# A two-layer decoder trunk on one core: norm rows asked for elsewhere, indices behind the first product, the first expert pair by halves

## The chip, the cores and the metric

The kernel runs on one core of one Trainium2 chip. A core has TensorE (PE: matrix products, with PEld for its weight loads), VectorE (DVE), ScalarE (ACT), GpSimd (POOL), the queue of SyncE (SP), and 16 DMA engines that move data between HBM and the on-chip memory. The metric is the device time of one execution in microseconds, the median of the runs.

## The reference

The reference is a decoder trunk of two layers for 256 tokens of 1024 features. Each layer mixes tokens (a gated linear recurrence in the first layer, stick-breaking attention in the second, both beside a softmax attention to 256 memory tokens), projects, adds and normalizes, and then applies a mixture of experts, adds and normalizes. Cut to the part that the change touches:

```python
mixed = jnp.concatenate([seq_out, mem_out], axis=-1)
x = post_norm(x, mixed @ w_o[layer], ln_mix_g[layer], ln_mix_b[layer])     # LN(alpha*x + out) * g + b
probs_g = softmax(xf @ w_group + b_group); p_top, g_idx = top_k(probs_g, 1)      # one of 4 groups
w_top, e_local = top_k(softmax(logits of that group), 2)                       # two of its 4 experts
h = silu(einsum('td,edf->tef', xf, w_gate)) * einsum('td,edf->tef', xf, w_up)   # 256 inner features
y = einsum('tef,efd->td', h * gates[:, :, None], w_down)                       # 16 experts
x = post_norm(x, y, ln_ffn_g[layer], ln_ffn_b[layer])
```

## The kernel before

The program is one unrolled stream of instructions per engine. A planner (the Tile scheduler) orders the instructions of each engine by program order and a simulated time; inside `tc.manual_schedule`, and for instructions given to `pin`, the written order stands. Tiles with one tag share a buffer, and a new tile waits for the readers of the old one.

**Weights.** All weights lie in one array of chunks of 1 MB. `Stream` (L54) sends them in order on SP's queue into free buffers: nine of a ring, and others that stages open for a time with `stream.open(names, end)`, for chunks below `end`. A chunk waits for the chunk that was sent three before it to land (DEPTH, L29, L96) and for its buffer. An expert pair has six chunks: four of gate and up weights (two halves of the 1024 features for each of two experts), two of down weights. The second layer's experts are the last 48 chunks; its last one is the last transfer of weights of the program.

**Routing, in `mixer_end`** (L937). TensorE finishes the output projection; VectorE adds the residual in four pieces (`add`, L399), two per tile of 128 tokens; `turn_in` (L561) transposes the sum four blocks at a time into PSUM, ScalarE copies them to `sT` (L567), and `logits` (L569) multiplies by the router's weights, while the norm's variance goes from VectorE (L409 or L423) to GpSimd, which raises it to the power -0.5 (L410, L424), and back to VectorE (L413, L427). `rank` and `pick` (L576, L593) on VectorE choose the experts, `count` (L600) on TensorE numbers the slots, `place` and `slots` (L607, L617) on VectorE build one-hot blocks `P0` (pair 0) and `P1` (all pairs). `z` (L960) writes the normalized rows to HBM. `gather_first` (L635) makes pair 0's transposed rows with products with `P0`, one call per tile of tokens. In the second layer the order of these on VectorE, TensorE and ScalarE is written by hand from L1016 to L1059.

**After it** (L1066 to L1081), `indices` (L653) multiplies all one-hot blocks by the token numbers (16 products of one column), VectorE makes integers of them, and GpSimd fetches pair 1 and 2 by indirect DMA. `first_rows` (L647) applies the norm's gain and bias to pair 0's eight blocks, four on ScalarE (L629) and four on VectorE (L627). `rows` (L376) brings the norm's two rows of 1024 into one partition of the tile `gb`, by ScalarE's queue, and GpSimd broadcasts each to 128 partitions (L384); with `by_transfer` one DMA of 1 MB repeats them instead (L380). `affine` (L432) multiplies and adds with them on VectorE.

**Experts, in `Moe.run`** (L803). Eight pairs of experts, 64 slots each. For each pair `gu` makes gate and up (512 columns, 256 of each, in one PSUM bank), 8 blocks of features by two experts; a product of 32-bit numbers runs as two instructions. ScalarE takes silu of the gate (L873), VectorE multiplies by up and by the slot's gate value (L875) to `h`; TensorE transposes `h` (L899), ScalarE copies it (L900), and the down products (L913) make two halves of 512 outputs. Pair 0 already takes ScalarE's and VectorE's work on `h` in two halves of 128 features. `turn` (L764) gets the gate values of a pair; `transpose_rows` (L782) turns the next pair's fetched rows. Pairs 5 to 7 are combined by products (L828), the others by way of HBM. All PE instructions of this part are pinned. `beyond` (L486) is for more than 64 tokens at an expert; every engine loads a number for it (L488), SP too.

The tile `gb` (tag "gb") is first the gate of the recurrence, then the norm rows, and in the second layer the value tile `vB` (read last by `so`, L1566). Slots "x0" and "x1" hold the layer's transposed input until the last projection has read it, and weights afterwards.

## Time and profile before

| | us |
|---|---|
| median of 3 runs | 525.6 (524.14 to 529.12) |
| the profiled execution, its own time | 526.96 |
| span of that execution, first to last instruction | 525.3 |
| TensorE busy | 491.1 |
| VectorE busy | 300.2 |
| ScalarE busy | 229.6 |
| GpSimd busy | 62.9 |
| data moved by DMA | 161.61 MB, 308 GB/s on the mean |

The profile lists each instruction with its start, counted from the first instruction, and its duration; an engine's idle time before an instruction stands in brackets with what ended it. The duration of a product contains its latency, so products in a row overlap and a row of several (x16) covers less than the sum. "issue" says that the engine waited for nothing that the profile shows. Issues of DMA stand on the queue of the engine that makes them (SPq, ACTq, POOLq), and their duration there is that of the issue, not of the transfer. The granted clock is a share of 2.4 GHz.

### The profile page before, as it was taken

How to read it: one execution, taken by the hardware profiler on the slowest of the kernel's cores; microseconds unless marked ns; L12 is line 12 of the kernel's file. 1: busy time of each engine (PE TensorE's matmuls, PEld its weight loads, DVE VectorE, ACT ScalarE, POOL GpSimd, SP SyncE). 2: the span in 40 equal slices, each digit the busy share in tenths (PEclk: the TensorE clock that was granted, in tenths of full speed). 3: DMA queues.
4: the chain of work that ended last, by engine and by line, in shares of the span. 5: the costliest groups of instructions: out<-in, count | busy, mean ns of one | idle time of the engine just before them, and what ended most of it. 6: DMA issues, size and time to landing. Idle time of an engine off the chain costs nothing. (4 is left out here: it accounts for less than half of the span.)

```text
span 525.3 us, 9096 instructions
## 1 busy us (share of the span) xinstructions
PE 491.1 (93%) x3534; PEld 326.7 (62%) x3534; DVE 300.2 (57%) x682; ACT 229.6 (44%) x471; POOL 62.9 (12%) x78
## 2 busy tenths in 40 slices
PE   4999999999999999999797999998998899999992
PEld 4998898788996333333236889877687333333431
DVE  4668876867758622233338698677445842233547
ACT  4845446684445222333017566668423232222322
POOL 1100000002132111112011500000010121111201
PEclk9999999999999999999898999999998999999997
DMA  8999834447888999999999763242999799999922
GB/s 270 407 404 404 345 103 160 161 156 326 299 332 321 384 403 384 394 385 407 409 379 395 271 252 143 100 160 99 381 365 364 288 382 419 414 422 409 412 119 81
DMA packets 28439, 161.61 MB, mean 308 GB/s; under 512 B 5239, under 2 KB 5623, under 8 KB 11363
## 3 DMA queue, kind: packets, MB, share of 16 engines
q1 hardware_dynamic: 20736, 140.76, 68.3%
q0 software_dynamic: 4752, 10.94, 5.4%
q10 hardware_dynamic: 2902, 9.26, 4.8%
q8 instruction: 30, 0.49, 0.4%
q14 instruction: 19, 0.16, 0.1%
HBM read 158.92 MB, written 13.64 MB: 329 GB/s over the span
## 5 line engine op out<-in xcount | busy, mean ns | idle before, releaser
L820 PE MATMUL gu<-w,ex 128*64 128x512 f32 x256 | 62.9, 609 | 3.4 <-DMA w<-in_w_all_dram 2.3
L820 PE MATMUL gu<-w,xg 128*64 128x512 f32 x256 | 60.8, 601 | 0.1
L913 PE MATMUL po<-w,hT 128*64 128x512 f32 (+1 forms) x272 | 58.4, 570 | 0.1
L913 PEld LDWEIGHTS po<-w,hT 128*64 128x64 f32 x272 | 18.8, 136 | 34.0 <-issue 27.3
L820 PEld LDWEIGHTS gu<-w,ex 128*64 128x64 f32 x256 | 17.2, 137 | 34.8 <-issue 26.1
L820 PEld LDWEIGHTS gu<-w,xg 128*64 128x64 f32 x256 | 16.4, 136 | 26.5 <-issue 24.6
L920 DVE COPY hr<-po 128x512 f32<-128x512 f32 x10 | 6.9, 692 | 43.1 <-PE po L913 43.0
L629 ACT ACTIVATE xg<-xgp,lnT 128x128 f32<-128x128 f32 x32 | 13.5, 457 | 25.6 <-PE xgp L791 22.4
L918 DVE TENSOR_TENSOR hl<-po,hl 128x512 fp32r<-128x512 f32 (+1 forms) x14 | 8.5, 615 | 26.5 <-ACT hl L917 25.5
L627 DVE TENSOR_SCALAR xg<-xgp,lnT 128x128 f32<-128x128 f32 x32 | 12.4, 408 | 19.0 <-ACT xg L629 15.7
L629 ACT ACTIVATE ex<-xgp,lnT 128x128 f32<-128x128 f32 x32 | 14.3, 458 | 19.3 <-PE xgp L791 19.0
L627 DVE TENSOR_SCALAR ex<-xgp,lnT 128x128 f32<-128x128 f32 x32 | 13.1, 410 | 15.1 <-ACT ex L629 13.9
L900 ACT ACTIVATE hT<-ht 128x256 f32<-128x256 f32 (+1 forms) x18 | 6.5, 360 | 34.4 <-PE ht L899 34.3
L873 ACT ACTIVATE h<-gu 128x256 f32<-128x256 f32 (+1 forms) x18 | 6.3, 360 | 34.3 <-PE gu L820 34.3
L234 DVE TENSOR_TENSOR wo<-w,wo 128x512 fp32r<-128x512 f32 x20 | 13.7, 727 | 10.8 <-ACT wo L226 10.8
L760 POOL DMA_INDIRECT hd<-hr,own x10 | 10.1, 1014 | 81.2 <-DVE gsl L780 76.3
L673 POOL DMA_INDIRECT zg<-zd,idx x14 | 14.6, 1041 | 43.2 <-PE xgp L791 25.1
L791 PEld LDWEIGHTS xgp<-cst,zg 128*128 128x128 f32 x112 | 12.0, 141 | 11.4 <-PE gu L820 7.3
L1291 POOL TENSOR_TENSOR rms<-rms,neghalf 128x2 f32<-128x2 f32 x6 | 4.1, 699 | 111.6 <-ACT sq L1287 99.4
L384 POOL PARTITION_BROADCAST gbm<-gbm x4 | 5.3, 1398 | 94.2 <-DMA gbm<-in_ln_dram 85.5
L226 ACT ACTIVATE wo<-w 128x512 fp32r<-128x512 f32 x20 | 11.5, 628 | 9.8 <-PE wo L472 8.2
L917 ACT ACTIVATE hl<-po 128x512 fp32r<-128x512 f32 (+1 forms) x14 | 7.5, 537 | 18.4 <-PE po L913 18.4
(462 smaller groups left out, 1357.7 us busy)
## 6 DMA issues: line engine op xcount, KB each, us to landing
w<-in_w_all_dram SPq DMA_DIRECT2D x131, 1024.0 KB
hd<-in_w_all_dram ACTq DMA_DIRECT2D x2, 2560.0 KB
w<-in_w_all_dram SPq DMA_DIRECT2D x6, 256.0 KB
x_tok<-in_x_tok_dram ACTq DMA_DIRECT2D x1, 1024.0 KB
zd<-z ACTq DMA_DIRECT2D x2, 512.0 KB
gbo<-in_ln_dram ACTq DMA_DIRECT2D x1, 1024.0 KB
out_dram<-z SPq DMA_DIRECT2D x4, 256.0 KB
w<-in_w_all_dram SPq DMA_DIRECT2D x1, 512.0 KB
```

The costliest lines, as they stand in the source:

```text
L226: self.last_hi = nc.scalar.activation(p[:, 0, s], src[:, s], AF.Copy, scale=1.0 if scale is None else scale).ins
L234: nc.vector.tensor_sub(p[:, 1, s], src[:, s], p[:, 0, s])
L627: ins = nc.vector.tensor_scalar(xg[:, kk], ps, g, b, op0=ALU.mult, op1=ALU.add)
L629: nc.scalar.activation(xg[:, kk], ps, AF.Identity, scale=g, bias=b)
L673: nc.gpsimd.indirect_dma_start(out=self.zg[:, p % 2], out_offset=None, in_=self.zd, in_offset=bass.IndirectOffsetOnAxis(ap=self.idx[:, p:p ...
L760: pin(nc.gpsimd.indirect_dma_start(out=self.hd, out_offset=bass.IndirectOffsetOnAxis(ap=self.own[:, p:p + 1], axis=0), in_=src, in_offset= ...
L791: pin(nc.tensor.transpose(ps[:, k], self.zg[:, p % 2, (4 * hk + k) * P:(4 * hk + k + 1) * P], ident))
L820: pin(nc.tensor.matmul(gus[p][c * 64:(c + 1) * 64], xgs[p][:, kk, c * CAP:(c + 1) * CAP], ws[p][2 * kh + c][0][:, k * 512:(k + 1) * 512], ...
L913: pin(nc.tensor.matmul(po[c * 64:(c + 1) * 64], hT[:, f, c * 64:(c + 1) * 64], ws[p][4 + c][0][:, f * D + s.start:f * D + s.stop], start=( ...
L917: self.hl_last = nc.scalar.activation(hl[:, 0, s], po, AF.Copy).ins
L918: pin(nc.vector.tensor_sub(hl[:, 1, s], po, hl[:, 0, s]))
L920: nc.vector.tensor_copy(hr[:, p % 2, s], po)
```

## The change

The diff has these parts.

- `rows` can fill a tile that is handed to it. The first layer's norm rows (of the mixer's norm) are asked for ahead of the load of `x_tok`; the second layer's by the repeating transfer, into slot "x1", behind the value projection and ahead of the output projection. `mixer_end` takes them as an argument, and no longer asks for them behind `first_rows`.
- In the second layer, "x1" is no longer opened for weights ahead of the output projection; "gb" is opened when the heads are done, and "x1" when `affine` has read it.
- `turn_in` copies the last of its four groups (second tile, second half) in two copies of two blocks.
- `first_rows` gives all eight blocks to ScalarE.
- `indices` is called behind the first block of pair 0's gate and up products, and its products are pinned.
- Pair 0's gate and up columns are read in the order gate, up, gate, up of 128 each (by the access pattern of the weights); the last four blocks of features are done first for the first 256 columns, then for the second 256.
- Pair 0's down products: both output halves with the first 128 inner features right behind the first half of `h`, with the second 128 behind the second half.

```diff
--- before.py
+++ after.py
@@ -373,9 +373,9 @@
     def tok_tile(which, name):
         return keep.tile([P, NT, D], F32, tag=which, name=name)
 
-    def rows(which, name, by_transfer=False):
-
-        gb = tok_tile("gb", f"gb{name}")
+    def rows(which, name, by_transfer=False, gb=None):
+
+        gb = tok_tile("gb", f"gb{name}") if gb is None else gb
         if by_transfer:
             nc.scalar.dma_start(gb, ln_d[0, 2 * which:2 * which + 2].partition_broadcast(P))
             return gb
@@ -562,9 +562,12 @@
 
             ps = bank(f"zt{self.l}", tag="y", shape=(P, 4, P))
             sT = self.sT[t, hk] = self.tmp.tile([P, 4, P], F32, tag="sT", name=f"sT{self.l}{t}", bufs=2)
+
+            n = 2 if t == hk == 1 else 4
             for k in range(4):
                 nc.tensor.transpose(ps[:, k], s[:, t, (4 * hk + k) * P:(4 * hk + k + 1) * P], ident)
-            nc.scalar.activation(sT, ps, AF.Copy)
+                if k % n == n - 1:
+                    nc.scalar.activation(sT[:, k + 1 - n:k + 1], ps[:, k + 1 - n:k + 1], AF.Copy)
 
         def logits(self, t, hk):
             if hk == 0:
@@ -647,7 +650,7 @@
         def first_rows(self):
             xg = self.work.tile([P, NK, P], F32, tag="xg", name=f"xg{self.l}")
             for k in range(NK):
-                self.features(xg, self.first[k // 4][:, k % 4], k, k // 4)
+                self.features(xg, self.first[k // 4][:, k % 4], k, 0)
             return xg
 
         def indices(self):
@@ -658,8 +661,8 @@
             ps = bank(f"idx{l}", tag="m", shape=(P, 8))
             for p in range(8):
                 for t in range(NT):
-                    nc.tensor.matmul(ps[:, p:p + 1], self.P1f[:, t, p * P:(p + 1) * P], tokb[:, t:t + 1], start=(t == 0),
-                                     stop=(t == 1))
+                    pin(nc.tensor.matmul(ps[:, p:p + 1], self.P1f[:, t, p * P:(p + 1) * P], tokb[:, t:t + 1],
+                                         start=(t == 0), stop=(t == 1)))
 
 
             pin(nc.vector.tensor_scalar(self.idx[:, 0:3], ps[:, 0:3], float(T), T - 1.0, op0=ALU.add, op1=ALU.min))
@@ -809,7 +812,7 @@
 
             quarters = [slice(0, 512), slice(512, 768), slice(768, D)]
 
-            def gu(p, ks):
+            def gu(p, ks, part=slice(0, 512)):
 
                 if p not in ws:
                     ws[p] = [stream.get() for _ in range(6)]
@@ -817,10 +820,13 @@
                 for kk in ks:
                     kh, k = kk // 4, kk % 4
                     for c in range(2):
-                        pin(nc.tensor.matmul(gus[p][c * 64:(c + 1) * 64], xgs[p][:, kk, c * CAP:(c + 1) * CAP],
-                                            ws[p][2 * kh + c][0][:, k * 512:(k + 1) * 512], start=(kk == 0),
-                                            stop=(kk == NK - 1)))
-                    if k == 3:
+                        w = ws[p][2 * kh + c][0][:, k * 512:(k + 1) * 512]
+                        if p == 0:
+                            w = w.rearrange("p (g h n) -> p h g n", g=2, h=2)
+                            w = w if part.stop - part.start == 512 else w[:, part.start // 256]
+                        pin(nc.tensor.matmul(gus[p][c * 64:(c + 1) * 64, part], xgs[p][:, kk, c * CAP:(c + 1) * CAP],
+                                            w, start=(kk == 0), stop=(kk == NK - 1), skip_group_check=(p == 0)))
+                    if k == 3 and part.stop == 512:
                         stream.done(ws[p][2 * kh][1], ws[p][2 * kh + 1][1])
 
             def combine(p, t, s):
@@ -835,10 +841,13 @@
 
             for p in range(8):
                 if p == 0:
-                    gu(0, range(4))
+                    gu(0, range(1))
+                    self.indices()
+                    gu(0, range(1, 4))
                     self.gates()
                     self.turn(0)
-                    gu(0, range(4, 8))
+                    for j in range(2):
+                        gu(0, range(4, 8), slice(256 * j, 256 * j + 256))
                     self.ex = slots.tile([P, 2, D], F32, tag="ex", name=f"ex{l}")
                 else:
 
@@ -869,11 +878,14 @@
                 h = pool.tile([P, 256], F32, name=f"h{l}")
 
                 parts = [slice(0, 256)] if p else [slice(0, P), slice(P, 256)]
-                for c in parts:
-                    nc.scalar.activation(h[:, c], gus[p][:, c], AF.Silu)
-                for c in parts:
-                    pin(nc.vector.scalar_tensor_tensor(h[:, c], gus[p][:, 256 + c.start:256 + c.stop],
-                                                       self.gsl[:, p:p + 1], h[:, c], op0=ALU.mult, op1=ALU.mult))
+
+                g = [c.start * (1 if p else 2) for c in parts]
+                n = 256 // len(parts)
+                for c, o in zip(parts, g):
+                    nc.scalar.activation(h[:, c], gus[p][:, o:o + n], AF.Silu)
+                for c, o in zip(parts, g):
+                    pin(nc.vector.scalar_tensor_tensor(h[:, c], gus[p][:, o + n:o + 2 * n], self.gsl[:, p:p + 1], h[:, c],
+                                                       op0=ALU.mult, op1=ALU.mult))
                 if p == 0:
                     self.turn(1)
                     yield None
@@ -892,12 +904,23 @@
                 if p == 7:
                     beyond(pool, self.pool, self.ex, l, base, self.x1, self.most, self.late, y)
                 hT = pool.tile([P, 2, P], F32, name=f"hT{l}")
+
+                def down(po, s, fs):
+                    for f in fs:
+                        for c in range(2):
+                            pin(nc.tensor.matmul(po[c * 64:(c + 1) * 64], hT[:, f, c * 64:(c + 1) * 64],
+                                                ws[p][4 + c][0][:, f * D + s.start:f * D + s.stop],
+                                                start=(f == 0), stop=(f == 1)))
+                pos = [bank(f"po{l}", tag="m") for _ in half] if p == 0 else []
                 for c in parts:
                     fs = slice(c.start // P, c.stop // P)
                     ht = bank(f"ht{l}", tag="m", shape=(P, 2, P))
                     for f in range(fs.start, fs.stop):
                         pin(nc.tensor.transpose(ht[:, f], h[:, f * P:(f + 1) * P], ident))
                     nc.scalar.activation(hT[:, fs], ht[:, fs], AF.Copy)
+                    if p == 0 and fs.start == 0:
+                        for po, s in zip(pos, half):
+                            down(po, s, (0,))
                 if 0 < p < 7:
                     gu(p + 1, range(2, 3))
                 if p > AWAY:
@@ -907,12 +930,8 @@
                     hl = keep.tile([P, 2, D], F32R, tag="v", name=f"hl{l}")
                 for hf, s in enumerate(half if p < 7 else quarters):
                     n = s.stop - s.start
-                    po = bank(f"po{l}", tag="m")[:, 0:n]
-                    for f in range(2):
-                        for c in range(2):
-                            pin(nc.tensor.matmul(po[c * 64:(c + 1) * 64], hT[:, f, c * 64:(c + 1) * 64],
-                                                ws[p][4 + c][0][:, f * D + s.start:f * D + s.stop],
-                                                start=(f == 0), stop=(f == 1)))
+                    po = pos[hf] if p == 0 else bank(f"po{l}", tag="m")[:, 0:n]
+                    down(po, s, (1,) if p == 0 else range(2))
                     if p >= AWAY:
                         self.hl_last = nc.scalar.activation(hl[:, 0, s], po, AF.Copy).ins
                         pin(nc.vector.tensor_sub(hl[:, 1, s], po, hl[:, 0, s]))
@@ -934,7 +953,7 @@
             self.y = y
 
 
-    def mixer_end(op, res, l, lasts, fill, finish):
+    def mixer_end(op, res, gb, l, lasts, fill, finish):
 
         tags[0] = "m"
         s = res
@@ -1066,16 +1085,14 @@
         tmp.release()
         work = tc.alloc_tile_pool(name=f"moe{l}", bufs=1, side="right", reuse_waits="tile")
         moe.start(work)
-        moe.indices()
         xg = moe.first_rows()
-        gb = rows(2 * l, f"m{l}")
         for p in moe.run(xg):
             if p == 0:
                 x1 = moe.x1 = tok_tile("u", f"x1{l}")
                 affine(x1, s, gb, ts=(0,))
             if p is None:
                 affine(x1, s, gb, ts=(1,))
-                stream.open(("gb",), end - 12, keep)
+                stream.open(*((("gb",), end - 12, keep), (("x1",), end))[l])
             if p == 6 + l:
                 gb = rows(2 * l + 1, f"o{l}", l == 1)
         tags[0] = "my"
@@ -1316,6 +1333,7 @@
         fl = op.main(range(3))
         weave(heads(), fl, 1)
         run(fl)
+    gb = rows(0, "m0")
     x_tok = tok_tile("v", "x_tok")
     nc.scalar.dma_start(x_tok, x_tok_d)
     stream.send(EXPERTS_END[0] - 48, keep, "u")
@@ -1451,7 +1469,7 @@
         stream.done(wk.chunk[1])
         wparts.use(*free)
         wparts.turn = 2
-    x2, gb, norms = mixer_end(op, x_tok, 0, [3], fl, into_next)
+    x2, gb, norms = mixer_end(op, x_tok, gb, 0, [3], fl, into_next)
 
 
     mixed = fpair("o", "mixB")
@@ -1550,7 +1568,8 @@
             weave(chain(sticks(range(8, 12)), mem_attn(pool, qm, 1, prs, mixed, place)), fl, 6 / 14)
             turned(11, betas.pop(11))
             run(fl)
-    stream.open(("x0", "x1"), EXPERTS_END[1])
+    gb1 = rows(2, "m1", True, slots.tile([P, NT, D], F32, tag="x1", name="gbm1"))
+    stream.open(("x0",), EXPERTS_END[1])
     wparts.use("wa", "wb", "wc", "wd")
     op = OutProj(mixed, 1)
     tags[0] = "m"
@@ -1571,6 +1590,7 @@
     next(fl)
     weave(heads(), fl, 0.5)
     run(fl)
+    stream.open(("gb",), EXPERTS_END[1] - 12, keep)
     stream.send(EXPERTS_END[1] - 48, keep, "u")
     stream.send(EXPERTS_END[1] - 47, slots, "ex")
     for q in (2, 3):
@@ -1608,7 +1628,7 @@
             gain(1, 1)
             bias(1, 0)
             bias(1, 1)
-    mixer_end(op, x2, 1, [2, 3], iter(()), into_output)
+    mixer_end(op, x2, gb1, 1, [2, 3], iter(()), into_output)
 
 
 # ---- launch: one core ----
```

## Rows read from the trace of the kernel before

**Rows 1.** The page's part 1: busy us, share of the span, instructions.
```profile
PE 491.1 (93%) x3534; PEld 326.7 (62%) x3534; DVE 300.2 (57%) x682; ACT 229.6 (44%) x471; POOL 62.9 (12%) x78
```

**Rows 2.** Timeline of PE, routing of layer two: start, us, instruction, count, [idle before].
```profile
397.52 0.96 PE L573 MATMUL lg<-rw,sT 128*128 128x20 f32 x8
398.97 0.18 PE L605 MATMUL slot<-Ab,trib 128*128 128x16 bf16 x1 [0.48 <-DVE Ab L597]
399.57 0.66 PE L566 MATMUL zt<-cst,z 128*128 128x128 f32 x4 [0.42 <-DVE z L399]
400.92 1.20 PE L573 MATMUL lg<-rw,sT 128*128 128x20 f32 x8 [0.69 <-ACT sT L567]
401.95 3.54 PE L644 MATMUL xgp<-P,z 128*128 128x128 f32 x16
...
406.24 2.02 PE L644 MATMUL xgp<-P,z 128*128 128x128 f32 x16 [0.71 <-DVE dl L690]
...
409.44 3.65 PE L820 MATMUL gu<-w,xg 128*64 128x512 f32 x16
```

**Rows 3.** Stages: busy us by engine (instructions), granted clock, DMA share, GB/s.
```profile
402.00:405.00 3.00, 3.00 (x15) 3.00 (x16) 1.67 (x9) 0.78 (x1) 0.00 (x0) 0.50 0.93 276
```

**Rows 4.** Timeline of DVE in the routing of layer two.
```profile
394.66 0.15 DVE L409 TENSOR_SCALAR normx<-normx 128x1 f32<-128x1 f32 x1 [1.32 <-ACT P L406]
396.73 0.16 DVE L413 TENSOR_TENSOR normx<-normx 128x1 f32<-128x1 f32 x1 [1.91 <-POOL normx L410]
...
398.83 0.68 DVE L399 SCALAR_TENSOR_TENSOR z<-z,wo 128x512 f32<-128x512 f32 x1
```

**Rows 5.** Timeline of POOL, whole span: two rows of layer one, one of two.
```profile
144.92 2.87 POOL L384 PARTITION_BROADCAST gbm<-gbm  x2 [8.70 <-issue]
155.87 0.59 POOL L410 TENSOR_TENSOR normx<-normx,neghalf 128x1 f32<-128x1 f32 x1 [8.07 <-issue]
...
396.10 0.59 POOL L410 TENSOR_TENSOR normx<-normx,neghalf 128x1 f32<-128x1 f32 x1 [10.61 <-issue]
```

**Rows 6.** Timeline of PE, pair 7 of the first layer.
```profile
254.79 3.57 PE L820 MATMUL gu<-w,ex 128*64 128x512 f32 x6 [2.30 <-DMA w<-in_w_all_dram]
```

**Rows 7.** Timeline of SP's queue in narrow windows of layer two: four weight transfers issued.
```profile
380.85 0.33 SPq L94 DMA_DIRECT2D w<-in_w_all_dram  x1
...
416.85 0.33 SPq L94 DMA_DIRECT2D w<-in_w_all_dram  x1
...
484.04 0.33 SPq L94 DMA_DIRECT2D w<-in_w_all_dram  x1
...
492.20 0.33 SPq L94 DMA_DIRECT2D w<-in_w_all_dram  x1
```

**Rows 8.** Timeline of PE, first products of pair 7 of the second layer.
```profile
493.06 1.89 PE L820 MATMUL gu<-w,ex 128*64 128x512 f32 x8
```

**Rows 9.** Timeline of ACT in the second layer, from routing to pair 1.
```profile
400.26 0.60 ACT L567 ACTIVATE sT<-zt 128x512 f32<-128x512 f32 x1 [2.04 <-PE zt L566]
...
408.30 1.50 ACT L629 ACTIVATE xg<-xgp,lnT 128x128 f32<-128x128 f32 x4 [1.41 <-PE xgp L644]
...
433.53 0.38 ACT L900 ACTIVATE hT<-ht 128x256 f32<-128x256 f32 x1 [1.73 <-PE ht L899]
```

**Rows 10.** Timeline of PE, first layer: index products and first gate and up products.
```profile
165.95 0.51 PE L661 MATMUL idx<-tokb,P 128*128 128x1 bf16 x15
166.58 3.65 PE L820 MATMUL gu<-w,xg 128*64 128x512 f32 x16
```

**Rows 11.** Timeline of PE at the end: pair 7's down products.
```profile
509.13 3.66 PE L913 MATMUL po<-w,hT 128*64 128x512 f32 x24
```

**Rows 12.** Timeline of PE, pair 0 of the second layer: transposes of h, down products.
```profile
417.79 0.65 PE L899 MATMUL ht<-cst,h 128*128 128x128 f32 x2 [0.80 <-DVE h L875]
418.48 1.94 PE L913 MATMUL po<-w,hT 128*64 128x512 f32 x8
```

**Rows 13.** Stages, columns as in rows 3: from gather to pair 0.
```profile
404.00:414.00 10.00, 8.78 (x67) 5.44 (x67) 7.57 (x38) 3.00 (x6) 1.88 (x2) 0.94 0.62 208
```

## The prediction

> **What bounds the kernel now.** I read the page's busy shares first: TensorE is busy for 491.1 us of 525.3 [rows 1]. A change can thus gain only where TensorE stands still or its clock is low; work added on VectorE, ScalarE or GpSimd costs only where TensorE waits for it. TensorE's list of waits and its timeline say where that is. In the second layer, between mixer and experts, it stands still three times in 2.4 us: 0.48 for the first tile's ranking, 0.42 for the sum of the second tile, 0.69 for ScalarE's copy of the turned sum [rows 2]. The stages view shows what follows: between 402 and 405 the granted clock is 0.50, the lower level of 1.2 GHz [rows 3], and the 16 gather products that take 2.02 us at 406.24 take 3.54 us at 401.95 [rows 2].
>
> The first of those waits starts on GpSimd. VectorE hands it the variance at 394.66; the power there starts at 396.10, after 10.61 us in which GpSimd waited for nothing that the profile shows, right behind the broadcast of the norm rows; VectorE goes on at 396.73 [rows 4, 5]. In the first layer the power stands idle for 8.07 us behind the same broadcast, and the broadcast for 8.70 us behind earlier powers [rows 5]. So going from power to broadcast, or back, costs GpSimd 8 to 10.6 us.
>
> The Trainium skill ("GPSIMD Engine Reference", 2.1 Instruction dispatch) says that the first call of a newly loaded GpSimd kernel pays a load of about 6 us that has no row of its own. The gaps here agree in kind, not in size. By 6 us from the broadcast's end the power would have been in time, and taking the broadcast away would be worth nothing.
>
> A second bound is the stream of weights. In the first layer TensorE waits 2.30 us for one transfer in pair 7, and the six products behind it take 3.57 us [rows 6], where 16 take 3.65 elsewhere [rows 2], so 1.4 would be due: its end is set by DMA. In the second layer it never waits for weights, but barely. Transfers go three deep (DEPTH), so the one issued at 484.04 has landed when that of 492.20 is issued [rows 7], and, counted back from the last, it is the one needed at 493.06 [rows 8]. The slack is 0.9 us.
>
> **The change part by part.** *Norm rows, first layer.* The request moves ahead of x_tok's load, but the tile that it fills is the gate's, read by the last head, and GpSimd's 8.70 us begin behind the last head's power. Neither moves: 0. If the order on ScalarE's queue pushed x_tok back, that would cost between nothing and one transfer, 2.7 us (three from 484.04 to 492.20 [rows 7]); x_tok can go as soon as v is free, before gb, so I take 0.
>
> *Norm rows, second layer.* The broadcast goes; 1 MB arrives by a repeating transfer in slot x1, asked for before the output projection. The power then starts when asked, at about 394.9 (394.66, 0.15 for the variance, a hand-over of 0.05) instead of 396.10: 1.2 us earlier. Behind it on VectorE stand the ranking of tile 0 and then the second tile's sum, at 398.83 [rows 4]. That sum also needs TensorE's last product, over when the logits start, 397.52, plus 0.2 of latency [rows 2]; so it starts at about 397.8, 1.0 us earlier, and the transposes at 398.5 instead of 399.57. The wait of 0.48 is gone, that of 0.42 nearly.
>
> *Copy by halves.* The logits start 1.35 us after the first transpose (399.57 to 400.92 [rows 2]), with a copy of 0.60 us between. A copy of half the width takes 0.38 [rows 9] and can start two transposes (0.25 us) sooner: 0.9 us. Logits at 399.4 instead of 400.92: 1.5 us so far. ScalarE pays 0.76 instead of 0.60, with nothing queued behind that TensorE waits for.
>
> *The clock.* The idle time ahead of the fall shrinks from 1.59 us to about 0.4, and I take it that the clock stays up. The first gather takes 2.0 instead of 3.54 us and ends at 402.4, 3.0 us earlier. The second gather also needs the second ranking, which follows the logits through a ranking chain that gains only 1.3 us, because the second variance now comes last in it; then a count and a one-hot block, together 0.9 us by my estimate from the wait of 0.71 and the count ahead of 406.24 [rows 2]. That puts it 0.3 behind the first gather's shift: 2.7 us earlier. If the clock fell all the same, 1.3 us would be left.
>
> *Features on ScalarE, indices behind the first product.* ScalarE makes four blocks in 1.50 us [rows 9], one each 0.38; TensorE uses one in 0.91 (16 instructions of 3.65 us are four blocks [rows 2]). With eight blocks there it still never waits: 0. The 16 index products cost 0.5 us (15 take 0.51 [rows 10]). In the first layer they fill the wait for the first feature block, and gu starts as soon as that is there, at 166.58 [rows 10]; behind the first product they fill it no longer: a loss of 0.5 us, ahead of pair 7's wait of 2.30 us for weights [rows 6] and so covered; without that cover it costs 0.5. In the second layer the gather ends 1.2 us before gu starts at 409.44 [rows 2]; from now on the first block takes 0.55 of them and the indices 0.5: gain 0.1. The fetch of pair 1's rows moves with them.
>
> *Pair 0 by halves.* Eight wide products become sixteen of half the width. The program's end shows the price: the 24 instructions at 509.13, 8 wide and 16 half wide, take 3.66 us [rows 11], so a half costs half. The read of weights in two pieces per product is not in the trace: between 0 and what the same pieces cost as products of their own, again 0 by that row. ScalarE and VectorE finish the first half of h under the second half's products (1.8 us), so the transposes of half 0 need not wait 0.80 us [rows 12]. But the new order puts transpose, copy, four down products (1.82 us), and only then the second transpose and copy, and each transpose and copy stand in front of TensorE for 0.69 us (417.79 to 418.48 [rows 12]). Now 1.65 us lie between gu's end (409.44, twice 3.65, the turn between) and 418.48; then 0.2 for the turn and twice 0.69. Gain 0.1 us, in the first layer covered again.
>
> *Slot x1 for gb.* One transfer of weights that went into x1 before the output projection waits for gb, free when the last heads are done, 380.85 [rows 7]: 2.7 us of DMA move behind it, and the norm rows fill the place it leaves. Between 404 and 414 DMA is busy for 0.62 of the time [rows 13], 3.8 us free, so it fits; but that gap shrinks as TensorE comes earlier. The next transfers are released by pair 0's products, at 416.85 [rows 7], so they move forward with TensorE. I take it that the stream moves forward by 2.5 us and the slack covers the rest: 0. The repeating transfer is issued on ScalarE's queue behind the last reader of x1; queued behind it are the splits of the output weights, which TensorE reads next. An issue holds SP's queue for 0.33 us [rows 7]; between 0 and that, I take 0.1.
>
> **Sum.** 2.7 + 0.1 + 0.1 − 0.1 = 2.8 us. The profiled execution took 526.96 us around its span of 525.3, 1.4 over the median of 525.6; so a profile near 524.2 and a median of 522.8.
>
> **Rivals.** *The clock falls all the same* (0.18): 1.3 + 0.1 = 1.4 us, 524.2. For it: the wait behind the first gather stays. Against: the wait of 0.80 us at 417.79 [rows 12] stands alone, and its products keep their pace. *The rows change nothing* (0.10): the power is late from another cause than the broadcast; the half copy's 0.45 and 0.1 remain, 525.0. Against: gaps of 8.07 and 10.61 us directly behind both broadcasts [rows 5]. The skill's 6 us would give this case. *The weights take it back, and more* (0.12, the other side): if the transfer put out of x1 isn't made good, everything behind it lands 2.7 us later, and the products of 493.06 start at 494.85 [rows 7, 8], 1.8 us later than now, after a wait of 4.6 us; behind that I expect the 2.2 us that six products lose in the first layer (3.57 less 1.4): 525.6 + 4.0 = 529.6. It decides from the point where the transfer of 416.85 is issued less than 1.9 us earlier; from there each microsecond is lost. *More than thought* (0.06): if the first layer's broadcast does come sooner, z and the stream with it start up to 2.6 us earlier, and pair 7's wait with its slow products (2.3 + 2.2) goes: with the 2.8, up to 7.3 us, 518 to 520.
>
> **How the numbers follow.** The likeliest (0.54) gives 522.8, its own range 521.3 to 524.3 (unknown costs of 0 to 0.5 us and the runs' spread). For 8 in 10 I add the two smaller gains and half of the way to the loss: 520.6 to 526.4. What a measurement of this kernel can tell from no change is about 1%, 5.3 us. Faster by more needs the last rival: 0.07. Slower by more, over 530.9, needs the third with another loss: 0.05. Within 1%: 0.88.
>
> **What would show it.** Right: no broadcast row on GpSimd in the second layer and its first power within 0.1 us of the variance; TensorE's waits in that routing under 0.5 us before the first gather; granted clock 1.00 through it; index products right behind the first four gu rows; in pair 0 two waits of about 0.55 us for copies in place of one of 0.80. Wrong: a wait of TensorE for weights in the second layer, a clock of 0.50 in its routing, or a first layer that ends at another time.

## The result, and the profile after

The changed kernel took 531.91 us (median of 18 runs, 529.13 to 541.84) against 525.92 of the kernel before beside it: a ratio of 1.0132, 95% interval 1.011 to 1.0155. It is slower by 1.3%, where 522.8 us and no measurable difference were forecast. The profiled execution took 533.31 us around a span of 531.6, against 526.96 and 525.3 before. The profiled executions of c_banks and c_gb below are 7 and 5 us longer than their medians, nearly all of it ahead of the second layer's routing, so only stretches of them are read.

TensorE's timeline of the changed kernel shows, in the second layer's routing, what was forecast; one line per group: start, duration, operation, and in brackets the idle time before it and what ended it.

```profile
397.85 0.44 PE L568 MATMUL zt<-cst,z 128*128 128x128 f32 x2
398.76 0.44 PE L568 MATMUL zt<-cst,z 128*128 128x128 f32 x2 [0.47 <-ACT sT L570]
399.03 1.26 PE L576 MATMUL lg<-rw,sT 128*128 128x20 f32 x8
400.14 2.03 PE L647 MATMUL xgp<-P,z 128*128 128x128 f32 x16
402.92 2.02 PE L647 MATMUL xgp<-P,z 128*128 128x128 f32 x16 [0.71 <-DVE dl L693]
405.49 1.08 PE L827 MATMUL gu<-w,xg 128*64 128x512 f32 x4 [0.55 <-ACT xg L632]
```

The three waits of [rows 2] ahead of the first gather have become one of 0.47, both gathers take 2.0 us, and pair 0 starts at 405.49 instead of 409.44. GpSimd's timeline has no broadcast, and its power follows VectorE's variance (394.03, 0.15 us) by 0.09 us:

```profile
394.27 0.55 POOL L410 TENSOR_TENSOR normx<-normx,neghalf 128x1 f32<-128x1 f32 x1 [97.36 <-DVE normx L409]
```

In pair 7, TensorE's timeline shows the loss. Before the change it never waited for weights in this layer:

```profile
488.04 2.79 PE L827 MATMUL gu<-w,xg 128*64 128x512 f32 x12
493.73 1.04 PE L827 MATMUL gu<-w,ex 128*64 128x512 f32 x2 [2.89 <-DMA w<-in_w_all_dram]
497.37 3.67 PE L827 MATMUL gu<-w,ex 128*64 128x512 f32 x6 [2.60 <-DMA w<-in_w_all_dram]
```

The stages view (columns: stretch, length, busy us and count of PE, PEld, DVE, ACT, POOL, then granted clock, DMA's busy share, GB/s) shows the clock's lower level from the second wait on, and two stretches in which DMA moves less:

```profile
420.00:440.00 20.00, 20.00 (x100) 7.31 (x100) 7.36 (x24) 6.09 (x14) 5.08 (x5) 1.00 0.98 386
440.00:460.00 20.00, 20.00 (x96) 6.61 (x92) 3.96 (x11) 4.54 (x11) 2.03 (x2) 1.00 0.97 369
...
494.80:501.60 6.80, 4.24 (x8) 1.29 (x9) 2.45 (x2) 0.00 (x0) 0.00 (x0) 0.50 1.02 419
```

SP's own list of waits, 400 to 505 (waiting line, what it waited for, us in total, times, longest), and SP's timeline show where the stream of weights stands. Before, the wait for `affine` was 3.1 us.

```profile
SPq L488 <- DVE G L714: 9.7, 1, 9.7
SPq L94 <- DVE x L440: 7.5, 1, 7.5
...
397.70 10.88 SPq L94 DMA_DIRECT2D w<-in_w_all_dram  x2
...
409.65 8.21 SPq L94 DMA_DIRECT2D w<-in_w_all_dram  x2
```

Each of the two timeline lines is one transfer at its start and one at its end, with nothing issued between: from 397.70 to 408.25 SP stands at the load of the number for `beyond` (L488), from 409.65 to 417.53 at a transfer into x1, which VectorE's `affine` frees. Chunks are numbered in the order in which they are needed; the last is 132. The numbers are those of the laid-out program; the trace shows only what each issue waited for. As the planner laid out SP's queue, it ran before the change 104, 103, load, 102, 105, 106, 107 (into gb), 108, 109, 110; in the changed kernel 104, load, 103, 102, **107** (into x1), 105, 106, 110, 108, 109. A queue goes on only when its first entry can: 105 and 106, whose buffers TensorE frees at the end of pair 0's gate and up, stood behind 107. And a chunk goes by the landing of the one three before it in the written order, so an order that isn't the written one also leaves fewer in flight later.

By stages of the second layer, worked out from the starts of these products in each profiled execution: from the layer's last attention product to pair 0's first product (routing), from there to pair 1's transposes of `h` (pair 0), from there to pair 7's (pairs 1 to 7). The last column is the ratio to the kernel before with its interval.

| kernel | routing | pair 0 | pairs 1 to 7 | wait for weights, pair 7 | ratio |
|---|---|---|---|---|---|
| before | 28.94 | 23.56 | 74.73 | 0 | 1 |
| changed | 25.62 | 25.12 | 83.52 | 5.5 | 1.0132 (1.011 to 1.0155) |
| a_order | 25.63 | 25.12 | 74.91 | 0 | 1.0009 (0.9965 to 1.0053) |
| a_107 | 25.62 | 25.11 | 75.56 | 0 | 1.0018 (0.9977 to 1.0058) |
| a_load | 27.24 | 25.12 | 82.53 | 3.9 | 1.012 (1.0052 to 1.0188) |
| b_order | 30.93 | 23.57 | 74.72 | 0 | 1.0035 (0.9997 to 1.0072) |
| a_norows | 31.99 | 25.11 | 74.73 | 0 | 1.0035 (1.0001 to 1.0069) |
| b_rows | 27.84 | 23.80 | 83.93 | 4.4 | 1.0087 (1.0028 to 1.0146) |
| c_best | 26.26 | 23.56 | 76.03 | 0 | 0.9965 (0.9922 to 1.0007) |

The span grew by 6.4 us: −3.3 in the routing, +1.6 in pair 0, +8.8 in pairs 1 to 7 (5.5 of waiting, most of the rest products at clock 0.50), −0.7 elsewhere.

### The profile page after: what moved, and what is told of

It is laid out like the page before. It is cut to its first block, busy times and chain, and to the rows that moved or that the text cites. A ratio compares the mean times of both kernels' runs of the same rounds, so it can differ in the third digit from the quotient of the medians.

```text
span 531.6 us, 9152 instructions
## 1 busy us (share of the span) xinstructions
PE 493.1 (93%) x3566; PEld 328.8 (62%) x3566; DVE 298.4 (56%) x674; ACT 232.8 (44%) x481; POOL 63.1 (12%) x76
## 5 line engine op out<-in xcount | busy, mean ns | idle before, releaser
L827 PE MATMUL gu<-w,xg 128*64 128x512 f32 (+1 forms) x288 | 61.5, 554 | 1.1 <-ACT xg L632 1.1
L827 PEld LDWEIGHTS gu<-w,xg 128*64 128x64 f32 x288 | 18.5, 136 | 24.7 <-issue 19.4
L632 ACT ACTIVATE xg<-xgp,lnT 128x128 f32<-128x128 f32 x40 | 16.3, 461 | 23.7 <-PE xgp L794 20.5
L630 DVE TENSOR_SCALAR xg<-xgp,lnT 128x128 f32<-128x128 f32 x24 | 9.7, 410 | 17.3 <-ACT xg L632 16.6
L794 PE MATMUL xgp<-cst,zg 128*128 128x128 f32 x112 | 15.3, 279 | 0.0
L941 ACT ACTIVATE hr<-po 128x512 f32<-128x512 f32 x10 | 6.0, 597 | 20.8 <-PE po L911 20.8
```

The costliest lines, as they stand in the source:

```text
L630: ins = nc.vector.tensor_scalar(xg[:, kk], ps, g, b, op0=ALU.mult, op1=ALU.add)
L632: nc.scalar.activation(xg[:, kk], ps, AF.Identity, scale=g, bias=b)
L794: pin(nc.tensor.transpose(ps[:, k], self.zg[:, p % 2, (4 * hk + k) * P:(4 * hk + k + 1) * P], ident))
L827: pin(nc.tensor.matmul(gus[p][c * 64:(c + 1) * 64, part], xgs[p][:, kk, c * CAP:(c + 1) * CAP], w, start=(kk == 0), stop=(kk == NK - 1), s ...
```

## The experiments

### Whose fault is the late stream?

**a_order**: the changed kernel, with the transfers from chunk 102 on in written order and the load of the number for `beyond` behind 104.

```diff
             ins = nc.sync.dma_start(t, w_all[i])
+            if i >= 102:
+                tc.keep_in_program_order(ins)
+            if i == 104:
+                self.ahead = ins
...
-        n = nc.values_load(most[0:1, 0:1], min_val=0, max_val=T)
+        loads, (n,) = nc.values_load_multi_w_load_instructions(most[0:1, 0:1], min_val=0, max_val=T)
+        for ld in loads:
+            if l and ld.ins.engine == mybir.EngineType.SP:
+                tc.add_manual_dep(ld.ins, stream.ahead.ins.name, mybir.DependencyInfo(
+                    mybir.DependencyClass.NoSync, mybir.DependencyReason.DATA), reason="load behind")
```

> The changed kernel with one thing different: on SP's queue the last transfers of weights (chunks 102 to 132) stand in the order in which they are written, and the second layer's load of the number for `beyond` stands behind chunk 104; every other engine's order is the same. Queue theory (the planner, seeing TensorE earlier, put chunk 103 behind that load and chunk 107, whose buffer VectorE frees at 417.5, ahead of 105 and 106, which TensorE had freed before; nothing was issued on SP from 397.70 to 408.25 and from 409.65 to 417.53): the two waits for weights in pair 7 (2.89 and 2.60 us) shrink under 0.5 us in all, the clock stays up behind them, and the time is 531.9 - 5.5 - 3.4 = 523.0, within 1.5. Traffic theory (1 MB more for the norm rows, 2.5 us at the 415 GB/s of the full stretches, and one buffer less for weights until 417): the waits stay at 3 us or more and the time at 530 to 533. Halves theory (pair 0 frees its weights later): the same, 530 to 533.

Measured: 526.66 us. No wait for weights is left in the second layer, and the clock stays at 1.00 until 514. In the stages view, against the 386 and 369 GB/s above:

```profile
420.00:440.00 20.00, 20.00 (x100) 7.28 (x98) 6.89 (x23) 5.08 (x12) 4.17 (x5) 1.00 1.01 419
440.00:460.00 20.00, 20.00 (x100) 6.79 (x97) 4.43 (x12) 4.53 (x10) 2.03 (x2) 1.00 1.01 416
```

The queue theory holds in that the order makes the loss: 1.3% is gone though the norm rows' 1 MB, the slots and pair 0 are as in the change. What in the order does it is the question of a_107 and a_load. The absolute forecast of 523.0 missed, since the kernel is then only as fast as before (527.14 beside it), not faster; the second group of experiments is about that.

**b_order**: the same edit on the kernel before.

> The kernel before with the same order written out on SP's queue (chunk 102 goes ahead of the load of the number for `beyond`, nothing else moves). All three theories: no wait for weights in the second layer either way, so within 1 us of before (525 to 526.5). If it gains 2 us or more, the order is worth something by itself, and the gain of the run above isn't the changed kernel's loss given back.

Measured: 528.78 us (before, beside it: 527.14), no wait for weights; the interval reaches to 1. The written order is worth nothing by itself. (Its routing is long because the clock fell there for longer, 0.66 on the mean from 396 to 411.)

**a_norows**: the changed kernel with the second layer's norm rows as before.

```diff
-    gb1 = rows(2, "m1", True, slots.tile([P, NT, D], F32, tag="x1", name="gbm1"))
-    stream.open(("x0",), EXPERTS_END[1])
+    stream.open(("x0", "x1"), EXPERTS_END[1])
...
-    stream.open(("gb",), EXPERTS_END[1] - 12, keep)
...
+        if l:
+            gb = rows(2, "m1")
```

> The changed kernel with the second layer's norm rows as before the change (one-partition load and broadcast on GpSimd into gb, behind the first rows; x1 opened for weights ahead of the output projection); copy by halves, features, indices and pair 0 by halves stay. On SP chunks 105, 106, 107 stand in that order again and 102 alone behind the load. Queue and traffic theories: no wait for weights over 0.5 us, about 525 (524 to 526.5). Halves theory: the waits in pair 7 stay, 529 or more.

Measured: 528.44 us, no wait for weights, so the halves are not what makes the stream late. It is some 3 us over the expected time (1.3 over the kernel before, beside it), and its routing is 3.1 us longer than before. The power again waits behind the broadcast, and TensorE behind the power (GpSimd's and TensorE's timelines):

```profile
380.33 2.87 POOL L384 PARTITION_BROADCAST gbm<-gbm  x2 [86.32 <-PE wo L472]
395.45 0.59 POOL L410 TENSOR_TENSOR normx<-normx,neghalf 128x1 f32<-128x1 f32 x1 [12.25 <-issue]
...
398.31 0.18 PE L608 MATMUL slot<-Ab,trib 128*128 128x16 bf16 x1 [3.37 <-DVE Ab L600]
```

**b_rows**: the kernel before with only the second layer's rows and slots changed (the three edits above, the other way).

> The kernel before with only the second layer's norm rows changed (by the repeating transfer into slot x1, gb and x1 opened for weights as in the change). On SP chunk 107 stands ahead of 105 and 106, and 103 and 102 behind the load, as in the changed kernel. Queue and traffic theories: waits for weights in pair 7 of 2 us or more, 528 to 532. Halves theory: no such waits, and the gain forecast for the rows alone, 525.6 - 2.5 = 523.1, within 1.

Measured: 529.09 us with 4.4 us of waiting for weights: the rows' part alone brings the loss.

**a_107** and **a_load** take the order apart. a_107 is a_order with `if i >= 105` and without the edit of the load; a_load leaves the transfers to the planner and puts the load behind 102, 103 and 104.

> The changed kernel with one thing different on SP's queue: from chunk 105 on the transfers stand in the order in which they are written, so 107, which waits for VectorE's `affine`, stands behind 105 and 106; the load of the number for `beyond` stays where the change put it, ahead of 103 and 102. Theory of the blocked head: the 7.5 us behind 107 are the cause; the waits for weights in pair 7 fall under 1 us in all, and the time is that of the run with the whole order written out, 526.7, within 1.5. Theory of the load: the 9.7 us in which SP stands at the load are the cause; the waits stay at 3 us or more, 530 to 533.

> The changed kernel with the other half of that order: the load of the number for `beyond` stands behind 104, 103 and 102; 107 stays ahead of 105 and 106. Theory of the blocked head: 103 and 102 go out some 8 us sooner, but nothing follows them until 417.5, so the stream is hardly ahead from there; the waits in pair 7 stay at 3 us or more, 529 to 533. Theory of the load: the waits fall under 1 us, 526.7 within 1.5.

Measured: a_107 526.82 us, a_load 532.49 (four runs). SP's list of waits and a line of its timeline in a_107, then SP's and TensorE's waits in a_load:

```profile
SPq L94 <- DMA w<-in_w_all_dram: 67.7, 25, 7.2
SPq L492 <- DVE G L718: 9.5, 1, 9.5
...
SPq L94 <- DVE x L444: 0.2, 1, 0.2
...
409.89 7.95 SPq L94 DMA_DIRECT2D w<-in_w_all_dram  x2
```

```profile
SPq L94 <- DVE x L442: 9.2, 1, 9.2
...
PE gu L834 <- DMA w<-in_w_all_dram: 3.9, 2, 2.5
```

In a_107 the load's 9.5 us are still there and the loss is gone, so the theory of the load falls. The theory of the blocked head has the right number, but not the mechanism: the wait for `affine` has gone from 7.5 to 0.2 us, and yet SP stands 7.2 us at the same place (the longest wait of the first line, and the timeline's line), now for an earlier transfer to land. It issues next at 417.51, in the changed kernel at 417.53. The difference comes behind that. SP's timeline over the next 15 transfers, in the changed kernel and in a_107:

```profile
417.53 42.40 SPq L94 DMA_DIRECT2D w<-in_w_all_dram  x15
```

```profile
417.51 37.46 SPq L94 DMA_DIRECT2D w<-in_w_all_dram  x15
```

In the order 107, 105, 106, 110, 108, 109 the same number of transfers takes 4.9 us longer. From 420 to 440 and from 440 to 460 a_107 moves 414 and 415 GB/s, the changed kernel 386 and 369. So the long wait that one sees at 107 is not the loss; the order of the transfers from there on is. That the rule of the chunk three before turns this order into lost time fits, but no run varies the rule. In a_load, where nothing else holds SP up there, the wait for `affine` is bare: DMA moves 72 GB/s from 415 to 420, at a busy share of 0.18. Its order behind that is the changed kernel's, and the loss stays. a_107 puts 105 and 106 back ahead of 107, and 108 and 109 ahead of 110; how much each of the two costs was not told apart.

### Why is there no gain once the stream is in time?

**c_banks**: a_order with pair 0's halves in two PSUM tiles.

```diff
                     gus[p] = bank(f"gu{l}", tag="y" if p <= AWAY else "m")
+                    if p == 0:
+                        gus[p] = [gus[p], bank(f"gv{l}", tag="y")]
...
+                            for j in range(part.start // 256, part.stop // 256):
+                                pin(nc.tensor.matmul(gus[0][j][c * 64:(c + 1) * 64, 0:256],
+                                                    xgs[p][:, kk, c * CAP:(c + 1) * CAP], w[:, j],
+                                                    start=(kk == 0), stop=(kk == NK - 1)))
```

> The run with the order written out on SP's queue, and pair 0's two halves of gate and up in two PSUM tiles (the first four blocks too are then multiplied by halves; all else the same). In the changed kernel ScalarE took silu of the first half only when the last product of the second was done (412.6, with 412.4 the products' end), and TensorE waited 0.81 us for it as before the change. Theory that one tile for both halves holds it back: ScalarE now starts under the second half's products, the 0.81 us falls under 0.1, pair 0 takes 24.3 instead of 25.1 us from its first product to pair 1's transposes, in both layers. Rival, that ScalarE or VectorE have other work in front: the wait stays at 0.5 or more. Time 526.7 - 0.8 to 1.6 = 525.1 to 525.9 by the first, 526.7 by the rival.

Measured: 525.3 us, ratio 0.9991 (0.9952 to 1.0029), by the time alone not told apart from a_order. ScalarE's timeline, first of a_order, then of c_banks, where the products of the second half run from 418.73 to 420.56:

```profile
412.57 0.45 ACT L893 ACTIVATE h<-gu 128x128 f32<-128x128 f32 x2 [4.48 <-PE gu L835]
```

```profile
418.95 0.28 ACT L899 ACTIVATE h<-gu 128x128 f32<-128x128 f32 x1 [3.26 <-PE gu L837]
420.70 0.28 ACT L899 ACTIVATE h<-gv 128x128 f32<-128x128 f32 x1 [1.48 <-PE gv L837]
```

In one tile both silus come behind the last product; in two, the first runs under the second half's products, and TensorE's wait of 0.81 us is gone. The two tiles are also two banks; whether two tiles in one bank would do, no run shows. Pair 0 takes 24.68 us in place of 25.12, half of what was expected: from the first product to the index products the first block by halves took 1.48 us where the whole one takes 1.01.

**c_best**: a_order without the pair 0 parts (products of gate and up and of down whole, as in the diff's removed lines), and with

```diff
+        moe.indices()
         xg = moe.first_rows()
...
-                    gu(0, range(1))
-                    self.indices()
-                    gu(0, range(1, 4))
+                    gu(0, range(4))
```

> The run with the order written out on SP's queue, without the parts in pair 0: whole gate and up products and down products as before the change, and the indices again ahead of the first product. What stays of the change is the norm rows, the copy by halves and the features on ScalarE. By the traces the halves cost pair 0 1.05 us (a wait of 0.81 as before, two copies of 0.37 and a transpose of 0.33 in front of TensorE where one transpose and copy of 0.69 stood) and the indices 0.5, in each of the two layers. If that is lost in both, the time is 526.7 - 3.1 = 523.6; if the weights take the first layer's part, 525.2. Rival: the pair 0 parts cost nothing that shows, 526 to 527.5.

Measured: 523.34 us, by the ratios 1.7% under the changed kernel; against the kernel before the interval just reaches 1, and it overlaps that of a_order. Pair 0 is back at 23.56 us in both layers (25.36 in the changed kernel's first), and the routing, indices included, is 2.7 us shorter than before. Pairs 1 to 7 take 1.3 us longer, 1.0 of it in pair 6, at granted clock 1.00. TensorE's timeline has there the eight products that took 1.89 us before [rows 8]:

```profile
487.37 2.68 PE L832 MATMUL gu<-w,ex 128*64 128x512 f32 x8
```

It looks as if TensorE has come so far forward that it meets the stream: in c_gb below, a wait of 0.55 us for weights stands between the second and the third of these eight. By the table the second layer's three stretches add up to 125.85 us here, to 125.66 in a_order and to 127.23 before. So, as far as one execution of each tells, what pair 0 gets back in the second layer the pairs behind it lose, and what c_best has over a_order is the first layer's part.

**c_best2** is c_best with 104 and 103 ahead of the load and of 102.

> The run without the pair 0 parts, with another order on SP's queue: 104 and 103 ahead of the load of the number for `beyond` and of 102, everything from 105 on as written. In the run before, 102 stood first and waited 10.2 us for the writing of z, with 103 and 104 behind it, and the DMA engines were busy for 0.78 of the time from 400 to 410; pair 6 then took 14.6 us where 13.6 is its time without waiting. If that is the stream, pair 6 falls to 13.6 and the time to 522.3; if not, it stays at 523.3.

Measured: 523.65 us, ratio 0.9965 (0.9925 to 1.0005). Pair 6 took 14.1 us, half of the way, and the time shows nothing of it: inconclusive.

**c_gb** is c_best with the rows brought into gb and x1 opened for weights as before the change.

```diff
-                stream.open(*((("gb",), end - 12, keep), (("x1",), end))[l])
+                stream.open(("gb",), end - 12, keep)
...
-    gb1 = rows(2, "m1", True, slots.tile([P, NT, D], F32, tag="x1", name="gbm1"))
-    stream.open(("x0",), EXPERTS_END[1])
+    stream.open(("x0", "x1"), EXPERTS_END[1])
...
-    stream.open(("gb",), EXPERTS_END[1] - 12, keep)
+    gb1 = rows(2, "m1", True)
```

> The run without the pair 0 parts, with the norm rows brought by the repeating transfer into gb, behind the heads, and x1 opened for weights ahead of the output projection as before the change: what the swap of the two slots costs. Theory that the order on SP was all: within 1 us of 523.3. Theory that the slot costs something beside: 1 to 2.5 us faster, no wait for weights and pair 6 in 13.6 in place of 14.6 us.

Measured: 523.07 us, ratio 0.9946 (0.9907 to 0.9985), half a per cent faster than the kernel before. Within 1 us of c_best: the swap of the two slots costs nothing that shows. Its pair 6 took 15.2 us at clock 1.00, so what holds pair 6 up is not the slots either.

**d_copy** (c_best with `n = 4`, the copy whole) and **d_two** (the last two of the four transposes into a tile of their own) are about the copy by halves.

> The run without the pair 0 parts (order on SP's queue written out, norm rows by transfer), with the last turned group copied whole as before the change. By its trace the copy by halves brings no time of its own: from the first transpose to the first gather product are 2.29 us, and 2.26 where the copy is whole. It splits one wait of 0.69 us into 0.47 and less. Theory that this keeps the clock up: with the whole copy the granted clock falls to 0.50 in the routing, as it did with the rows alone, the first gather takes 3.66 in place of 2.03 us, and from the last attention product to pair 0's first product are 27.8 in place of 26.3 us; the time is 523.3 + 1.5 = 524.8. Theory that it is worth nothing: the clock stays up and the stretch within 0.3 us of 26.3.

> The same run, with the last turned group in two PSUM tiles of two blocks each instead of one of four. TensorE waited 0.47 us between its second and third transpose for ScalarE's copy of the first two blocks. Theory that one tile holds both (the third transpose writes the tile that the copy still reads): that wait is gone, the stretch from first transpose to first gather product falls from 2.29 to 1.8 us, the time by 0.5. Rival: the wait moves to the logits, the stretch stays at 2.2 or more.

Measured: d_copy 523.86 us, ratio 0.9966 (0.9923 to 1.0009); d_two 523.03, 0.9966 (0.992 to 1.0012). TensorE's timeline in d_copy, and a stage:

```profile
398.24 1.07 PE L584 MATMUL lg<-rw,sT 128*128 128x20 f32 x8 [0.69 <-ACT sT L578]
...
399.00:404.00 5.00, 4.29 (x27) 4.17 (x27) 3.12 (x18) 1.31 (x2) 0.00 (x0) 0.66 0.97 355
```

The clock fell, and its routing takes 27.54 us in place of 26.26, as the clock theory said. The time doesn't show it: pairs 1 to 7 take 74.99 us in place of 76.03, so that most of it is given back. One execution is thin, but the others agree for the most part. With the rows by transfer and the copy whole (b_rows, d_copy) the clock fell both times; with the copy by halves in one tile it stayed at 1.00 in seven executions of eight, and fell in a_load (0.66 from 399 to 404, the first gather 3.42 us). In d_two the transposes follow each other and the first gather comes earlier, but not the second:

```profile
395.38 0.44 PE L578 MATMUL zt<-cst,z 128*128 128x128 f32 x2
395.66 0.38 PE L578 MATMUL zu<-cst,z 128*128 128x128 f32 x2
396.30 1.07 PE L586 MATMUL lg<-rw,sT 128*128 128x20 f32 x8 [0.25 <-ACT sT L580]
397.21 2.03 PE L657 MATMUL xgp<-P,z 128*128 128x128 f32 x16
...
400.36 0.46 PE L657 MATMUL xgp<-P,z 128*128 128x128 f32 x2 [0.68 <-DVE dl L703]
```

The stretch is 1.83 us, as expected, but the second gather waits for VectorE's ranking of the second tile, and the routing (26.15) is as long as in c_best.

## Why the prediction was wrong, step by step

**The stream, the step that failed.** "I take it that the stream moves forward by 2.5 us and the slack covers the rest: 0." It took the order on SP's queue as it stood. With x1 given to the norm rows the planner put 107, whose buffer `affine` frees, ahead of 105 and 106, and 110 ahead of 108 and 109; why it did, no run shows. The stream did not move forward: the transfer of 416.85 [rows 7] became one of 417.53. This alone costs nothing, since a_107 issues at 417.51 and TensorE never waits. The step should have had a price for a new order: 15 transfers take 42.40 us instead of 37.46, and two stretches of 20 us move 386 and 369 GB/s where a_order moves 419 and 416, which makes 1.6 MB. TensorE then waits 5.5 us.

The rival "The weights take it back, and more" came near (a wait of 4.6 us and 529.6 in all), but by luck. Its sign came true, the transfer of 416.85 not being issued earlier; its mechanism, a transfer put out of x1 and not made good, did not: a_order has the same slots and the same transfers, and no wait.

**Norm rows, second layer: right.** The power follows within 0.1 us, and the last turned group starts 1.1 us earlier, as forecast, counted from the last attention product (380.50 before, 379.87 after). With the copy and the clock it makes the routing 2.7 us shorter with the indices in their old place; forecast for the three was 2.7. a_norows shows the other side, 12.25 us between broadcast and power. The Trainium skill ("GPSIMD Engine Reference", 2.1 Instruction dispatch) gives about 6 us for the first call of a newly loaded kernel. By that the power would have been in time; a_norows rules it out here, where the broadcast ends at 383.20, VectorE has the variance at 391.26 and the power starts at 395.45.

**Copy by halves: wrong in what it saves.** From the first transpose to the logits 0.9 us were forecast in place of 1.35, a gain of 0.45. They take 1.18 us with the halves (397.85 to 399.03) and 1.34 with the copy whole (b_rows), and the first gather comes no sooner: 2.29 us after the first transpose, and 2.26. The third transpose waits 0.47 us for the copy, since both are in one PSUM tile; and d_two shows that without that wait the second ranking sets the end. The 2.7 us came out all the same, since the forecast took them from the second ranking and not from the first gather. What the copy does bring is the clock, in seven executions of eight: "I take it that the clock stays up" held in the changed kernel, but with the copy whole it did not.

**Pair 0 by halves: wrong in sign.** "ScalarE and VectorE finish the first half of h under the second half's products" was taken without asking where the halves lie: in one PSUM tile. So the wait of 0.8 stayed and the two copies came on top: 25.12 us instead of 23.56, of which the indices are 0.5. The Trainium skill ("PSUM — Partial Sum Buffer", PSUM bank collisions raise a hardware error) says that TensorE's write and another engine's access to the same bank and partitions must not coincide and are to be kept apart by bank, not by address. By that rule the first half could not be read early; the trace agrees, with the silu at 412.57 in one tile and under the products in two.

**Features and indices: right in the second layer** (TensorE waits 0.55 us for the first block, and the index products cost 0.5 behind it); in the first they cost the same 0.5, as forecast for the case without cover.

**First layer: "covered" was wrong.** The cover was pair 7's wait of 2.30 us [rows 6], from one execution. From pair 0's first product to pair 7's transposes the first layer took 105.03 us there, but 100.78 and 99.37 in b_order and b_rows, with the same work in that stretch; with the halves it took 101.24 to 102.34 (five executions), in c_best, c_best2, d_copy and d_two 99.46 to 100.67. Only c_gb's execution has such a wait again (3.1 us, 104.72 in all). So the halves and the moved indices cost some 1.8 us there too, which pair 0's own stretch shows as well (25.36 against 23.56).

**The sum as it was**, a_order against the kernel before: in the second layer −3.3 in the routing (−2.7 for rows, copy and clock, the rest for the indices moved out of it), +1.6 in pair 0 (about 1.05 for the halves, 0.5 for the indices) and +0.2 behind it; in the first layer +1.8. This leaves a_order where the kernel before is. In the changed kernel come 5.5 us of waiting and the slow products behind it on top.

## What to carry to other kernels

Where a planner orders a queue, a change of buffers is also a change of that order: read the new order of the transfers' queue, which entry waits for whom, before the stream is costed at nothing. The longest wait on a queue need not be the loss: in a_107 SP waits nearly as long at the same place, and nothing is lost. Work in halves overlapped here only where the halves lay in different PSUM tiles. And a wait that is to hide a cost must be there in more than one execution.

## What was not expected of the hardware

The order of equal transfers on one queue, with the program letting at most three in flight, changed what DMA moved over 40 us from about 417 (a_order) or 414 (a_107) to 378 GB/s, at a busy share of 0.97 to 0.98 against 1.01 to 1.02: the share hardly shows it. The granted clock fell to 0.50 (1.2 GHz) behind a single wait of 0.69 us in d_copy and b_rows, and stayed at 1.00 (2.4 GHz) behind one of 0.47 in the changed kernel, a_order, a_107, c_banks, c_best, c_best2 and c_gb; but in a_load it fell behind 0.47 as well.
